# A two-layer hybrid backbone on one core: equal tile addresses modulo 512, plain-order Hyena gates, and a first posts tile partly from SBUF

## The chip, the core and the metric

The kernel runs on one core of a Trainium2 chip. The engines are called PE (TensorE, the matrix engine; PEld is its loading of weights), DVE (VectorE), ACT (ScalarE), POOL (GpSimd) and SP (SyncE, which issues most DMAs). The metric is the device time of one execution in microseconds, as the median of several runs; a trace of one profiled execution shows where it goes.

## The reference

Two layers over 1024 tokens of width 1024, all in float32. Layer 0 has a mixer of two halves with one input and one output projection: RG-LRU heads (512 channels) and order-2 Hyena channels (512). Layer 1 has a Conformer convolution module. Each layer ends in an expert-choice MoE: 16 experts, each takes its top 128 tokens. What the change touches, cut to its core:

```python
# layer 0, mixer
proj = h @ p['w_in']                       # gate | xa_raw | hy (three pieces of 512)
y_a = gelu(gate) * (hs[0] + flip(hs[1]))   # RG-LRU half
u = dwconv1d(hy, ...)                      # short filter, three taps
v, *gates = split(u, 3)
z = v
for o in range(2):
    z = gates[o] * fftconv(z, kf[:, o], filt_bias[o])
out = concat([y_a, z]) @ p['w_out']
# each layer, MoE
xs = h[idx]                                # the 128 tokens of each of 16 experts
y = (silu(xs @ w1) * (xs @ w3)) @ w2 * gates
```

## The kernel before

**Products.** Nearly every product of the kernel is three matmuls: `mm3` (L155 to L158) multiplies a high part and a low part of both operands, hi x hi (L156), hi x lo (L157), lo x hi (L158), each with a stationary tile of 128x128 and a streamed tile of 128x512. `split` (L160 to L162) makes the two parts: ACT casts the high part, DVE subtracts it and leaves the residual. In the trace these lines stand for all their callers, so tiles' names tell them apart: `e` and `th`, `tl` are weights and tokens of the experts, `oh`, `ol` the output projection's weights, `wh`, `wlo` the input projection's and the conformer's. A few products remain plain float32 matmuls (L1275 with `wx` or `w` and `xf`).

**The layer-0 mixer.** `proj` gives one 128-channel piece of the input projection for all 1024 tokens in PSUM. `gate` (two pieces early, two at the mixer's end) applies gelu (L742, ACT), multiplies by the recurrent half (L743, DVE) and stores the piece `ge` to a DRAM tensor `ycd` (L744), rows 0 to 3 of its seven-piece part. `short` does the short filter of a Hyena piece: one ACT row (L786) and two DVE rows (L787, L788). The long convolution of a 128-channel quarter works through a Fourier transform of 1024 = 8 x 128 points: `tok` transposes the piece (PE, L668, eight tiles read with a stride of 8 elements, and two ACT copies `ut`, L669); `hy_fwd` is 16 matmuls and copies `y4` (L615); `hy_st1` eight DVE rows (L622, L623); `hy_mid` an 8-point transform of 16 rows (L584 to L601), the product with the filter's spectrum and its first butterflies (L633 to L640), and the 16 rows again; `hy_inv` 16 matmuls into two PSUM tiles (L651); `hy_gate` two DVE products (L659), which multiply a PSUM tile in order (a, p) by the gate piece `y` read as `q (p a) -> q a p`, a stride of 8 elements, and write the result `zt` with the same stride. Each of the four quarters goes through it twice (order 0, then order 1): sixteen products. The result of order 0 goes through `tok` again, that of order 1 to `ycd` rows 4 to 6; the last quarter's stays in SBUF. The order of the instructions on PE, DVE and ACT comes from a scheduler, from the posts' first tile on from the code.

**The posts.** The output projection runs over eight tiles of 128 tokens. `y_load` (L935) brings seven channel pieces of a tile from `ycd`, `split` makes `th` and `tl` of them (128x896), the eighth piece `zh`, `zl` comes from the last quarter. Tile 0's 48 matmuls are written with the mixer's last steps: load of `yc`, two wide splits of the weights (`wide_hi` L987 on ACT, `wide_lo` L992 on DVE), the last `drain` (inverse and gate), the splits, the remaining wide splits. After each tile's products come DVE rows (L1049, L1050) and the routing's logits; a top-128 sort for the routing runs on DVE behind them. The same posts code serves layer 1, with tiles `sTh` and `sTl`.

**The experts and the end.** 16 experts per layer; an expert gathers its tokens, has three products with 1024x1024 weights, split on the fly, and scatters. `final` adds the last expert's output per token tile (`ohT`, `hi`, `lo`) and applies the last norm; it has small tiles `ss`, `ms`, `rs` of one column each.

**Addresses.** SBUF tiles are laid out by pools in the order in which they are opened. So a small tile's size shifts the start of all that comes behind it, the tiles of the products among them. `route_open` opens the pool with `gates` and `pos`, which stays for the rest of its layer.

Of the kernel before, what the change touches and what calls it, by code (L numbers as in the profile page):

```python
# [9 lines left out]
F32 = mybir.dt.float32  # L10
# [5 lines left out]
OP = mybir.AluOpType  # L16
# [132 lines left out]
class Builder:  # L149
# [141 lines left out]

    def rstd(self, pool, ss, n=1):
        nc = self.nc
        m = pool.tile([128, n], F32, name="ms", tag="ms", bufs=4)
        nc.vector.tensor_scalar(m, ss, 1.0 / D, EPS, op0=OP.mult, op1=OP.add)  # L295
        r = pool.tile([128, n], F32, name="rs", tag="rs", bufs=4)
        nc.gpsimd.tensor_tensor(r, m, self.nh[:, :n], op=OP.pow)  # L297
        return r
# [354 lines left out]

    def hy_gate(self, p, J):
        dst = p.tile([128, D], F32, name="zt", tag="zt", bufs=1)
        zv = dst.rearrange("q (p a) -> q a p", a=8)
        gv = J["gate"].rearrange("q (p a) -> q a p", a=8)
        for h, q in enumerate(J["r"]):
            self.nc.vector.tensor_tensor(zv[:, h * 4:h * 4 + 4], q, gv[:, h * 4:h * 4 + 4], op=OP.mult)  # L659
        return dst  # L660

    def to_tok(self, src, dst):
        nc = self.nc
        for h in range(2):
            q = self.ps.tile([128, 4, 128], F32, name="q", tag="n")
            for j in range(4):
                a = h * 4 + j
                nc.tensor.transpose(q[:, j], src[:, a::8], self.idn)  # L668
            nc.scalar.copy(dst[:, h * 4:h * 4 + 4, :], q)  # L669

    def even_mixer(self, st, so):
# [7 lines left out]
        with ExitStack() as s1, ExitStack() as sl:  # L679
# [57 lines left out]
            def gate(p, ct, tag, n):  # L737
                P = proj(*piece(ct * 128))
                hs = p.tile([128, n], F32, name="hsr", tag=tag, bufs=4 if tag == "cv" else 2)[:, :D]
                nc.sync.dma_start(hs, self.hsd[ct * 128:(ct + 1) * 128, :])  # L740
                ge = p.tile([128, n], F32, name="ge", tag=tag, bufs=4 if tag == "cv" else 2)[:, :D]
                nc.scalar.activation(ge, P, AF.Gelu_apprx_tanh, bias=0.0, scale=1.0)  # L742
                nc.vector.tensor_tensor(ge, ge, hs, op=OP.mult)  # L743
                nc.sync.dma_start(self.ycd[ct * 128:(ct + 1) * 128, :], ge)  # L744

            with ExitStack() as s2:
# [44 lines left out]
            def tok(y):  # L791
                ut = py.tile([128, 8, 128], F32, name="ut", tag="u", bufs=2)
                self.to_tok(y, ut)
                return ut

            pend = []

            def drain():
                J = pend.pop(0)
                self.hy_inv(py, J)  # L800
                z = self.hy_gate(py, J)
                if J["o"] == 0:
                    return tok(z)
                i = J["qd"]
                if i == 3:
                    return z
                nc.sync.dma_start(self.ycd[512 + i * 128:512 + (i + 1) * 128, :], z)

            for i in range(4):
                J0 = dict(o=0, qd=i, u=tok(short(i)))  # L810
                if i == 0:
# [9 lines left out]
                self.hy_mid(py, J0)  # L821
                J0["gate"] = short(4 + i)
                self.fill(4)
                g1 = short(8 + i)
                pend.append(J0)
                J1 = dict(o=1, qd=i, u=drain(), gate=g1)
                self.hy_fwd(py, J1)
# [5 lines left out]
            self.ada_todo = [(1, 2, k) for k in range(8)]  # L833
            for ct in (2, 3):
                gate(py, ct, "cv", D)
            sl.close()
# [8 lines left out]
            with tc.tile_pool(name="pq0", bufs=1, reuse_waits="tile") as pq, \  # L845
                    tc.manual_schedule(engines={mybir.EngineType.PE, mybir.EngineType.DVE, mybir.EngineType.Activation}):
                y = self.y_load(pq, 0, 1)
                th = pq.tile([128, 7, 128], F32R, name="th")
# [7 lines left out]
                z = drain()  # L856
                self.split(th, tl, y)
                self.split(self.zh, self.zl, z)
# [64 lines left out]
    def route_open(self, l, st):  # L923
        tc = self.tc
        self.pr = pr = st.enter_context(tc.tile_pool(name=f"pr{l}", bufs=1, reuse_waits="tile"))
        self.gates = pr.tile([128, NE], F32, name="gates")
        self.pos = pr.tile([128, 8, NE], F32, name="pos")
# [15 lines left out]
    def mix_open(self, l, st, st2):  # L943
# [17 lines left out]
        E.memset(self.R2, 0.0)  # L961
        self.cb = pm.tile([128, NE], F32, name="cb")

# [523 lines left out]
    def ln_stats(self, Y, bst, pc):  # L1487
# [14 lines left out]
        self.ln_last = getattr(op, "ins", op)  # L1502
        rs = pc.tile([128, 16], F32, name="lrs")
        for a, b in ((0, 2), (2, 6), (6, 11), (11, 16)):
# [66 lines left out]
    def final(self, pe, y, g2b, wx):  # L1571
# [8 lines left out]
        for t in range(8):  # L1580
# [13 lines left out]
            j = pe.tile([128, D], F32, name="sa", tag="sa", bufs=1)  # L1594
            ss = pe.tile([128, 1], F32, name="ss", tag="ss", bufs=4)
            nc.scalar.activation(j, z, AF.Square, bias=0.0, scale=1.0, accum_out=ss)
            V.scalar_tensor_tensor(x, z, self.rstd(pe, ss), wx[0][:, 0], op0=OP.mult, op1=OP.mult)  # L1597
            nc.sync.dma_start(self.out[t * 128:(t + 1) * 128, :], x)
# [95 lines left out]
```

## Time and profile before

| | before |
|---|---|
| median of 3 runs | 2282.1 us (2279.15 to 2284.48) |
| the profiled execution | 2282.96 us |
| its span | 2281.2 us |
| mean granted clock of TensorE | 0.963 |

Times within the trace count from the span's start. The stages lie as follows: preparation and the recurrent half to about 300 us, the Hyena quarters from there to 541 us, the posts of layer 0 to about 690 us, its experts from about 700 us, the conformer from about 1290 us, the posts of layer 1 from about 1520 us, its experts from about 1690 us to the end. A busy engine need not be the one that sets a stage's length: that is read from the waits.

### The profile page before, as it was taken

What the parts mean: (1) busy time and instruction counts of PE and PEld (TensorE: products, weight loads), DVE (VectorE), ACT (ScalarE), POOL (GpSimd) and SP (SyncE); (2) the same over time, 40 slices, a digit from 0 to 9 for tenths busy, and PEclk for the clock granted to TensorE, in tenths of its full rate; (3) what the DMA queues carried; (4) which work ended last, traced back from release to release, by engine and by line L of the source; (5) the groups of instructions that cost most, each with busy time, mean ns of one, the idle gap of its engine ahead of it and who ended that gap; (6) DMA issues with size and microseconds to landing.
All of it is one profiled execution on the core that took longest, in us unless ns stands there. A gap on an engine that the chain in (4) does not pass through costs nothing.

```text
span 2281.2 us, 28699 instructions
## 1 busy us (share of the span) xinstructions
PE 2121.9 (93%) x10626; PEld 1654.5 (73%) x10626; DVE 1818.4 (80%) x2874; ACT 1201.7 (53%) x1459; POOL 129.9 (6%) x131
## 2 busy tenths in 40 slices
PE   7999998988967999999999899989689999999997
PEld 5976766757754877878778588877457777777775
DVE  5979799997596989899888624186969898888887
ACT  3658621212214777777777521134247767676774
POOL 0000000000001000000000100010010000000001
PEclk9999998988988999999999899989889999999999
DMA  7241573654848999999998744334779999999974
GB/s 275 110 139 47 188 274 121 230 203 138 306 155 325 367 394 378 394 380 375 396 381 307 244 148 139 120 109 179 261 292 364 388 368 387 373 372 382 370 267 157
DMA packets 210021, 616.09 MB, mean 270 GB/s; under 512 B 27988, under 2 KB 76758, under 8 KB 200089
## 3 DMA queue, kind: packets, MB, share of 16 engines
q1 hardware_dynamic: 198610, 572.84, 66.2%
q0 software_dynamic: 11248, 41.42, 7.3%
q8 instruction: 83, 1.36, 0.2%
q14 instruction: 56, 0.46, 0.1%
q10 hardware_dynamic: 24, 0.01, 0.0%
HBM read 558.62 MB, written 55.61 MB: 269 GB/s over the span
## 4 chain that ended last, share of the span: by engine, by line
PE 63%; DVE 5%; issue 1%; DMA 1%; POOL 0%; ACT 0%; POOLq 0%; ACTq 0%
PE P L156 17%; PE P L158 17%; PE P L157 17%; PE P L1275 6%; PE q L1240 3%; PE q L1415 1%; DMA xs<-h2d,ix 0%; DVE W L909 0%; DVE wx L1597 0%; POOL rs L297 0%; DVE mm L893 0%; DVE Y L1435 0%; PE q L235 0%; DVE h L1059 0%; DVE S L906 0%
## 5 line engine op out<-in xcount | busy, mean ns | idle before, releaser
L162 DVE TENSOR_TENSOR e<-wx,e 128x1024 fp32r<-128x1024 f32 x516 | 617.9, 1223 | 86.9 <-ACT e L161 73.9
L161 ACT CAST e<-wx 128x1024 fp32r<-128x1024 f32 x516 | 540.2, 1051 | 226.1 <-PE P L158 224.1
L156 PE MATMUL P<-e,th 128*128 128x512 f32 x1384 | 562.9, 407 | 0.0
L158 PE MATMUL P<-e,tl 128*128 128x512 f32 x1384 | 543.5, 393 | 0.8 <-DVE tl L162 0.8
L157 PE MATMUL P<-e,th 128*128 128x512 f32 x1384 | 543.2, 392 | 0.0
L157 PEld LDWEIGHTS P<-e,th 128*128 128x128 f32 x1384 | 260.3, 188 | 60.9 <-DVE e L162 3.8
L156 PEld LDWEIGHTS P<-e,th 128*128 128x128 f32 x1384 | 260.1, 188 | 60.8 <-issue 7.2
L158 PEld LDWEIGHTS P<-e,tl 128*128 128x128 f32 x1384 | 259.9, 188 | 59.9 <-DVE tl L162 1.2
L162 DVE TENSOR_TENSOR e<-w,e 128x1024 fp32r<-128x1024 f32 x176 | 211.7, 1223 | 48.8 <-ACT e L161 29.6
L156 PE MATMUL P<-hh,wh 128*128 128x512 f32 x576 | 228.8, 398 | 16.2 <-DVE y L788 12.8
L161 ACT CAST e<-w 128x1024 fp32r<-128x1024 f32 x176 | 183.9, 1051 | 92.7 <-PE P L158 73.4
L157 PE MATMUL P<-hl,wh 128*128 128x512 f32 x576 | 228.9, 397 | 0.4 <-DVE ms L295 0.4
L158 PE MATMUL P<-hh,wlo 128*128 128x512 f32 x576 | 227.6, 396 | 0.1
L156 PEld LDWEIGHTS P<-hh,wh 128*128 128x128 f32 x576 | 108.9, 189 | 49.8 <-issue 23.7
L157 PEld LDWEIGHTS P<-hl,wh 128*128 128x128 f32 x576 | 109.2, 190 | 27.1 <-issue 4.3
L158 PEld LDWEIGHTS P<-hh,wlo 128*128 128x128 f32 x576 | 108.7, 189 | 26.2 <-issue 3.9
L1315 POOL DMA_INDIRECT acc<-yo,ix x31 | 50.7, 1634 | 923.9 <-DVE yo L1314 923.9
L162 DVE TENSOR_TENSOR tl<-q,th 128x512 fp32r<-128x512 f32 x128 | 84.8, 685 | 5.2 <-ACT th L161 4.1
L161 ACT CAST wh<-w 128x1024 fp32r<-128x1024 f32 x16 | 16.7, 1048 | 124.1 <-PE P L157 124.1
L1275 PE MATMUL P<-wx,xf 128*128 128x512 f32 x176 | 79.1, 592 | 0.0
L161 ACT CAST th<-q 128x512 fp32r<-128x512 f32 x128 | 71.8, 587 | 1.7 <-PE q L1240 1.7
L297 POOL TENSOR_TENSOR rs<-ms,nh 128x1 f32<-128x1 f32 x42 | 24.2, 577 | 825.0 <-issue 435.9
(415 smaller groups left out, 3030.0 us busy)
## 6 DMA issues: line engine op xcount, KB each, us to landing
wx<-i_exp_w SPq DMA_DIRECT2D x272, 1024.0 KB, 8.1
w<-i_exp_w SPq DMA_DIRECT2D x96, 1024.0 KB, 7.6
w<-i_w_mod SPq DMA_DIRECT2D x40, 1024.0 KB, 7.8
wst<-i_w_in SPq DMA_DIRECT2D x20, 512.0 KB, 4.4
kd<-w SPq DMA_DIRECT2D x8, 1024.0 KB, 5.0
w<-kd SPq DMA_DIRECT2D x8, 1024.0 KB, 8.6
acc<-res SPq DMA_DIRECT2D x16, 512.0 KB, 2.9
e<-i_exp_w SPq DMA_DIRECT2D x16, 512.0 KB, 7.7
```

The lines of the kernel that those rows point to most:

```text
L156: t.matmul(o, lh, rh, start=start, stop=False)
L157: t.matmul(o, lh, rl, start=False, stop=False)
L158: t.matmul(o, ll, rh, start=False, stop=stop)
L161: self.nc.scalar.copy(hi, src)
L162: self.nc.vector.tensor_sub(lo, src, hi.bitcast(F32))
L297: nc.gpsimd.tensor_tensor(r, m, self.nh[:, :n], op=OP.pow)
L1240: nc.tensor.transpose(q[:, j], src[:, c * 128:(c + 1) * 128], self.idn)
L1275: nc.tensor.matmul(P[:, ns], f[:, k], h[:, ns], start=k == 0, stop=k == 7)
L1315: self.last = nc.gpsimd.indirect_dma_start(self.acc[l][:, :], bass.IndirectOffsetOnAxis(ap=xT[e][1][:, 0:1], axis=0), yo, None, compute_op ...
L1415: op = nc.tensor.matmul(q[64 * half:64 * half + 64, gr % 4], U2[half][:, gr], TT[half][:, gr], start=True, stop=True, tile_position=(0, 64 ...
```

## The change

Three edits stand in one diff.

1. Sizes of small tiles are changed, without a use of what is added: `gates` of layer 1 gets 40 more columns, `cb` 16, `lrs` 120, and the small tiles of `final` move to another ring of buffers. The start addresses behind them shift. The table has, for the streamed and the stationary tile of a product, the difference of their start addresses modulo 512 bytes, from the allocation in either program.

| products | matmuls | before | after |
|---|---|---|---|
| experts of layer 0 (`e`; `th`, `tl`) | 692 x 3 | 0 | 0 |
| experts of layer 1 (`e`; `th`, `tl`) | 692 x 3 | 224 | 0 |
| experts of layer 1, plain float32 (`wx`; `xf`) | 44 | 224 | 0 |
| posts of layer 0, tile 0, and piece 7 of all | 10 x 3 and more | 0 | 0 |
| posts of layer 0, tiles 1 to 7 (`oh`, `ol`; `th`, `tl`) | 98 x 3 | 448 | 0 |
| posts of layer 1 (`oh`, `ol`; `sTh`, `sTl`) | 128 x 3 | 320 | 0 |
| conformer (`wh`, `wlo`; `hh`, `hl`) | | 0 | 0 |

2. The Hyena gate is permuted once by ACT (`hy_perm`, eight copies of 128x1024), so that the gate product reads and writes in plain order. The transposes behind an order-0 product read its result in plain order. For order 1, quarters 0 to 2, ACT copies the result back to the stride-8 order (`zs`, three copies) before its store. The last quarter's order-1 products still write with the stride. Both new tiles share a ring of four buffers with `y`, `ge` and `hsr`.

3. The first posts tile takes pieces 2 and 3 from the SBUF tiles that `gate` returns; the load of `yc` covers pieces 0, 1 and 4 to 6 in two DMAs, and the split is done in four parts (two, one, one and three pieces).

```diff
     def hy_gate(self, p, J):
+        nc = self.nc
         dst = p.tile([128, D], F32, name="zt", tag="zt", bufs=1)
-        zv = dst.rearrange("q (p a) -> q a p", a=8)
-        gv = J["gate"].rearrange("q (p a) -> q a p", a=8)
+        last = J["o"] == 1 and J["qd"] == 3
+        zv = dst.rearrange("q (p a) -> q a p", a=8) if last else dst.rearrange("q (a p) -> q a p", a=8)
         for h, q in enumerate(J["r"]):
-            self.nc.vector.tensor_tensor(zv[:, h * 4:h * 4 + 4], q, gv[:, h * 4:h * 4 + 4], op=OP.mult)
-        return dst
+            nc.vector.tensor_tensor(zv[:, h * 4:h * 4 + 4], q, J["gate"][:, h * 4:h * 4 + 4], op=OP.mult)
+        if J["o"] == 0 or last:
+            return dst
+        z = p.tile([128, D], F32, name="zs", tag="cv", bufs=4)
+        nc.scalar.copy(z.rearrange("q (p a) -> q a p", a=8), zv)
+        return z
+
+    def hy_perm(self, p, y):
+        g = p.tile([128, D], F32, name="ga", tag="cv", bufs=4).rearrange("q (a p) -> q a p", a=8)
+        self.nc.scalar.copy(g, y.rearrange("q (p a) -> q a p", a=8))
+        return g
...
-                nc.tensor.transpose(q[:, j], src[:, a::8], self.idn)
+                nc.tensor.transpose(q[:, j], src[:, a], self.idn)
...
-                J0["gate"] = short(4 + i)
+                J0["gate"] = self.hy_perm(py, short(4 + i))
...
-                J1 = dict(o=1, qd=i, u=drain(), gate=g1)
+                J1 = dict(o=1, qd=i, u=drain(), gate=self.hy_perm(py, g1))
...
-                y = self.y_load(pq, 0, 1)
+                y = pq.tile([128, 7, 128], F32, name="yc")
+                yv = self.ycd.rearrange("(k p) t -> p k t", p=128)[:, :, 0:128]
+                for a, b in ((0, 2), (4, 7)):
+                    nc.sync.dma_start(y[:, a:b], yv[:, a:b])
...
-                self.split(th, tl, y)
+                for a, b, part in ((0, 2, y[:, 0:2]), (2, 3, ges[0][:, None, :128]), (3, 4, ges[1][:, None, :128]), (4, 7, y[:, 4:7])):
+                    self.split(th[:, a:b], tl[:, a:b], part)
...
-        self.gates = pr.tile([128, NE], F32, name="gates")
+        self.gates = pr.tile([128, NE + (40 if l else 0)], F32, name="gates")[:, :NE]
...
-        self.cb = pm.tile([128, NE], F32, name="cb")
+        self.cb = pm.tile([128, 2 * NE], F32, name="cb")[:, :NE]
...
-        rs = pc.tile([128, 16], F32, name="lrs")
+        rs = pc.tile([128, 136], F32, name="lrs")[:, :16]
...
-            ss = pe.tile([128, 1], F32, name="ss", tag="ss", bufs=4)
+            ss = pe.tile([128, 1], F32, name="ss", tag="ix", bufs=6)
...
-            V.scalar_tensor_tensor(x, z, self.rstd(pe, ss), wx[0][:, 0], op0=OP.mult, op1=OP.mult)
+            V.scalar_tensor_tensor(x, z, self.rstd(pe, ss, tag="ix", bufs=6), wx[0][:, 0], op0=OP.mult, op1=OP.mult)
```

In the code of the change lines below the gates stand some ten to seventeen further down (gate product L660, copy-back L664, permutation L669, transposed tile L679, gelu L752, its product L753, short filter L797 to L799, wide splits L1004 and L1009). How the order moves is seen at three places.

DVE at the mixer's end, before. `L600`, `L601` are the last transform rows, `L743` the second gelu product, `L992` the wide residuals, `L659` the last gate pair, `tl` and `zl` the residuals of tile 0.

```order
L600 SCALAR_TENSOR_TENSOR pq<-sub,E 128x2x128
L601 SCALAR_TENSOR_TENSOR pq<-sub,E 128x2x128
L743 TENSOR_TENSOR ge<-ge,hsr 128x1024
L992 TENSOR_TENSOR ol<-w,oh 128x2048 x2
L659 TENSOR_TENSOR zt<-q,y 128x4x128 x2
L162 TENSOR_TENSOR tl<-yc,th 128x896
L162 TENSOR_TENSOR zl<-zt,zh 128x1024
L992 TENSOR_TENSOR ol<-w,oh 128x2048 x2
```

All wide residuals and the second gelu product stand behind the transform there; the first gelu product stood ahead of it.

DVE there with the change, first ahead of the last transform's 16 rows (`L639`, `L640` are the butterflies directly ahead of them).

```order
L753 TENSOR_TENSOR ge<-ge,hsr 128x1024
L637 TENSOR_TENSOR sub<-E,w 128x1024
L1009 TENSOR_TENSOR ol<-w,oh 128x2048
L638 TENSOR_TENSOR pq<-pq,sub 128x8x128
L753 TENSOR_TENSOR ge<-ge,hsr 128x1024
L639 TENSOR_TENSOR E<-pq 128x1024
L640 TENSOR_TENSOR E<-pq 128x1024
```

Both gelu products stand among the rows of the filter product, and one wide residual does. Behind the last transform, on DVE with the change:

```order
L601 SCALAR_TENSOR_TENSOR pq<-sub,E 128x2x128
L1009 TENSOR_TENSOR ol<-w,oh 128x2048
L660 TENSOR_TENSOR zt<-q,ga 128x4x128 x2
L162 TENSOR_TENSOR tl<-yc,th 128x256
L162 TENSOR_TENSOR tl<-ge,th 128x128 x2
L162 TENSOR_TENSOR tl<-yc,th 128x384
L162 TENSOR_TENSOR zl<-zt,zh 128x1024
L1009 TENSOR_TENSOR ol<-w,oh 128x2048 x2
```

One wide residual is left between the transform and the gate pair, and tile 0's residual comes in four parts.

ACT at the mixer's end, before (gelu, wide casts, cast of tile 0).

```order
L286 COPY w<-q 8x256
L742 ACT_TABLE_LOAD
L742 ACTIVATE ge<-P 128x1024 x2
L987 CAST oh<-w 128x2048 x3
L161 CAST th<-yc 128x896
L161 CAST zh<-zt 128x1024
L987 CAST oh<-w 128x2048
```

Both gelu rows stand together, and one row casts tile 0.

The same with the change.

```order
L752 ACT_TABLE_LOAD
L752 ACTIVATE ge<-P 128x1024
L286 COPY w<-q 8x256
L1004 CAST oh<-w 128x2048
L752 ACTIVATE ge<-P 128x1024
L1004 CAST oh<-w 128x2048 x2
L161 CAST th<-yc 128x256
L161 CAST th<-ge 128x128 x2
L161 CAST th<-yc 128x384
L161 CAST zh<-zt 128x1024
L1004 CAST oh<-w 128x2048
```

A wide cast stands between the two gelu rows now, and the cast of tile 0 comes in four parts, of which two read `ge`.

DVE around a gate pair of order 0 in the second quarter, before: the end of a transform, residuals of the weight split (`wlo`), the gate pair, then the rows behind a forward transform.

```order
L600 SCALAR_TENSOR_TENSOR pq<-sub,E 128x2x128
L601 SCALAR_TENSOR_TENSOR pq<-sub,E 128x2x128
L162 TENSOR_TENSOR wlo<-wst,wh 128x1024 x2
L659 TENSOR_TENSOR zt<-q,y 128x4x128 x2
L622 TENSOR_TENSOR pq<-q,y_2877 128x256
```

Two residuals stand between the transform and the gate pair.

The same with the change.

```order
L600 SCALAR_TENSOR_TENSOR pq<-sub,E 128x2x128
L601 SCALAR_TENSOR_TENSOR pq<-sub,E 128x2x128
L799 SCALAR_TENSOR_TENSOR y<-P,vec,y 128x1023
L162 TENSOR_TENSOR wlo<-wst,wh 128x1024
L660 TENSOR_TENSOR zt<-q,ga 128x512 x2
L622 TENSOR_TENSOR pq<-q,y_2887 128x256
```

One of the two `wlo` rows went ahead, and the short filter's second row stands there; the gate pair has the plain form. On ACT the new copies of that quarter stand between the rows of the short filter.

```order
L664 COPY zs<-zt 128x8x128
L797 ACTIVATE y<-P,vec 128x1024
L161 CAST wh<-wst 128x1024
L669 COPY ga<-y 128x1024
L797 ACTIVATE y<-P,vec 128x1024
L669 COPY ga<-y 128x1024
L679 COPY ut<-q 128x512 x2
L615 COPY y_3364<-q 128x256
```

The copy-back `zs` is ahead of a short filter's row, and the permutations `ga` are behind one each, the second of them ahead of the transposed tile. On PE, the inverse of such an order-0 gate had two and two projection matmuls directly ahead of it and has 28 and 13 now, the 13 between its fourth and fifth matmul; this is so in three quarters.

## Rows read from the trace of the kernel before

**Rows 1.** The page, busy time of each engine, share of the span, instructions.

```profile
PE 2121.9 (93%) x10626; PEld 1654.5 (73%) x10626; DVE 1818.4 (80%) x2874; ACT 1201.7 (53%) x1459; POOL 129.9 (6%) x131
```

Columns of a window: its bounds, its length, busy microseconds of each engine with its records, the granted clock of TensorE as a share of full speed, the mean busy share of the DMA engines, and what they moved in GB/s.

**Rows 2.** Windows of twelve experts: layer 0, layer 1; length, then each engine's busy time.

```profile
730.40:1156.40 426.00, 426.00 (x1970) 338.06 (x1969) 385.28 (x372) 312.81 (x336) 30.85 (x24) 1.00 1.01 383
1696.40:2131.40 435.00, 435.00 (x1970) 338.56 (x1969) 385.58 (x373) 312.72 (x336) 30.84 (x24) 1.00 1.01 374
```

A row gives shortest, median and longest duration in ns, and the first and the last start.

**Rows 3.** Timeline of line L1275 on PE, layer 0 then layer 1, grouped.

```profile
L1275 PE MATMUL P<-wx,xf x64: 590/592/592, 730.5 to 1088.5; 128*128 128x512 f32 x64
...
L1275 PE MATMUL P<-wx,xf x64: 591/592/593, 1696.4 to 2061.9; 128*128 128x512 f32 x64
```

A row of this view gives line, engine, operation, output and inputs, shapes, count; then busy microseconds and mean ns of one; then idle time of the engine ahead of it.

**Rows 4.** Groups by form, three-pass matmuls of twelve experts, layer 0 then 1.

```profile
L157 PE MATMUL P<-e,th 128*128 128x512 f32 x528 | 205.9, 390 | 0.0
...
L157 PE MATMUL P<-e,th 128*128 128x512 f32 x529 | 209.0, 395 | 0.0
```

**Rows 5.** Groups by form: layer-0 posts, layer-1 posts, conformer.

```profile
L157 PE MATMUL P<-ol,th 128*128 128x512 f32 x72 | 28.4, 395 | 0.0
...
L157 PE MATMUL P<-ol,sTh 128*128 128x512 f32 x88 | 34.6, 394 | 0.0
...
L157 PE MATMUL P<-hl,wh 128*128 128x512 f32 x122 | 47.6, 390 | 0.0
```

**Rows 6.** Windows of the layer-0 posts, columns as in rows 2.

```profile
570.00:590.00 20.00, 19.94 (x117) 14.79 (x116) 10.48 (x14) 6.34 (x12) 1.10 (x2) 1.00 0.93 309
630.00:650.00 20.00, 19.11 (x101) 14.88 (x101) 19.09 (x99) 3.32 (x6) 0.55 (x1) 1.00 0.40 132
```

**Rows 7.** Windows of the Hyena stage, columns as in rows 2.

```profile
300.00:541.40 241.40, 216.32 (x1238) 162.65 (x1236) 225.21 (x405) 46.84 (x73) 0.00 (x0) 0.94 0.53 191
360.00:380.00 20.00, 11.35 (x49) 9.44 (x49) 17.60 (x27) 0.59 (x1) 0.00 (x0) 0.57 0.42 142
```

**Rows 8.** Groups by form: Hyena gates, a plain PSUM product, an ACT cast.

```profile
L659 DVE TENSOR_TENSOR zt<-q,y 128x512 f32<-128x512 f32 x14 | 15.4, 1121 | 4.7 <-PE q L651 4.7
...
L1049 DVE TENSOR_TENSOR y<-P,g1b 128x512 f32<-128x512 f32 x6 | 4.1, 692 | 15.0 <-PE P L158 14.8
...
L161 ACT CAST wh<-wst 128x1024 fp32r<-128x1024 f32 x10 | 10.5, 1052 | 67.9 <-PE P L157 67.9
```

A row gives who waited and for whom; total microseconds, times, the longest.

**Rows 9.** Waits of DVE, 290 to 565 us.

```profile
DVE pq L622 <- ACT y L615: 9.8, 5, 2.7
DVE zt L659 <- PE q L651: 4.7, 5, 1.3
```

A row gives start, duration, engine, line, operation, and in brackets the engine's idle time before it and what ended that.

**Rows 10.** Timeline of the mixer's end: DVE, PE, ACT, SP's queue.

```profile
541.29 1.22 DVE L743 TENSOR_TENSOR ge<-ge,hsr 128x1024 f32<-128x1024 f32 x1
542.43 4.49 DVE L992 TENSOR_TENSOR ol<-w,oh 128x2048 fp32r<-128x2048 f32 x2
546.83 2.04 DVE L659 TENSOR_TENSOR zt<-q,y 128x512 f32<-128x512 f32 x2
552.51 1.09 DVE L162 TENSOR_TENSOR tl<-yc,th 128x896 fp32r<-128x896 f32 x1 [3.64 <-ACT th L161]
...
541.43 5.02 PE L651 MATMUL q<-IG,pq 128*128 128x128 f32 x28 [2.52 <-DVE pq L601]
552.53 0.80 PE L156 MATMUL P<-oh,th 128*128 128x512 f32 x1 [6.08 <-ACT th L161]
...
558.09 0.63 PE L156 MATMUL P<-oh,th 128*128 128x512 f32 x1
...
565.45 0.39 PE L157 MATMUL P<-ol,zh 128*128 128x512 f32 x1
...
566.36 0.39 PE L158 MATMUL P<-oh,zl 128*128 128x512 f32 x1
...
551.54 0.94 ACT L161 CAST th<-yc 128x896 fp32r<-128x896 f32 x1 [6.63 <-DMA yc<-ycd]
...
547.76 0.37 SPq L935 DMA_DIRECT2D yc<-ycd  x1
```

More of the change, by code (lines that the diff above doesn't have):

```diff
@@ L290, in bcast, with rstd @@
         self.nc.sync.dma_start(dst, self.rowd[l][i:i + 1, :].to_broadcast([128, D]))
-    def rstd(self, pool, ss, n=1):
+    def rstd(self, pool, ss, n=1, tag=None, bufs=4):
         nc = self.nc
-        m = pool.tile([128, n], F32, name="ms", tag="ms", bufs=4)
+        m = pool.tile([128, n], F32, name="ms", tag=tag or "ms", bufs=bufs)
         nc.vector.tensor_scalar(m, ss, 1.0 / D, EPS, op0=OP.mult, op1=OP.add)
-        r = pool.tile([128, n], F32, name="rs", tag="rs", bufs=4)
+        r = pool.tile([128, n], F32, name="rs", tag=tag or "rs", bufs=bufs)
         nc.gpsimd.tensor_tensor(r, m, self.nh[:, :n], op=OP.pow)
@@ L744, in gate @@
                 nc.sync.dma_start(self.ycd[ct * 128:(ct + 1) * 128, :], ge)
+                return ge
             with ExitStack() as s2:
@@ L794, in tok, with split8 @@
                 return ut
+            def split8(y):
+                return y.rearrange("q (p a) -> q a p", a=8)
             pend = []
@@ L802, in drain @@
                 if J["o"] == 0:
-                    return tok(z)
+                    return tok(z.rearrange("q (a p) -> q a p", a=8))
                 i = J["qd"]
@@ L809, in even_mixer @@
             for i in range(4):
-                J0 = dict(o=0, qd=i, u=tok(short(i)))
+                J0 = dict(o=0, qd=i, u=tok(split8(short(i))))
                 if i == 0:
@@ L833, in even_mixer @@
             self.ada_todo = [(1, 2, k) for k in range(8)]
-            for ct in (2, 3):
-                gate(py, ct, "cv", D)
+            ges = [gate(py, ct, "cv", D) for ct in (2, 3)]
             sl.close()
```

## The prediction

> **What bounds the kernel now.** I read the busy line of the page first: PE is busy 2121.9 us of the 2281.2 us span, so a gain has to shorten PE's work or one of the stretches in which PE waits [rows 1]. Then I went through the three stretches that the change touches.
>
> The experts are PE alone: in twelve expert periods of either layer PE is busy 426.00 of 426.00 us and 435.00 of 435.00 us, at granted clock 1.00, with the same 1970 matmul records, DVE and ACT below and the DMA engines equally occupied [rows 2]. Yet layer 1 takes 9.0 us more, 0.75 us per expert. A matmul that comes once per period tells the same: ten periods are 1088.5 - 730.5 = 358.0 us in layer 0 and 2061.9 - 1696.4 = 365.5 us in layer 1 [rows 3]. The excess sits in the three-pass matmuls, whose mean is 390 ns in layer 0 and 395 ns in layer 1 [rows 4], while the plain float32 matmuls have 592 ns in both [rows 3]. By the tile addresses of the program, the streamed tile and the stationary tile start 0 bytes apart modulo 512 in layer 0 and 224 apart in layer 1.
>
> The Hyena stage (300 to 541.4 us) is DVE's: 225.21 us busy of 241.40, PE 216.32, ACT only 46.84, granted clock 0.94 [rows 7]. At the mixer's end DVE, the y load and PE hand over to each other, row by row [rows 10]. The posts behind it are PE's at first (19.94 of 20 us) and then as much DVE's, because of the sort (19.09 us in 630 to 650) [rows 6].
>
> The profiled execution took 2282.96 us, span 2281.2; the median of the runs is 2282.1. I sum against 2282.96; the 0.9 us between the two is small beside the terms.
>
> **A. Layer-1 experts.** Padding takes the difference of their 692 x 3 three-pass matmuls from 224 to 0, what layer 0 has. 16 experts x 0.75 us = 12.0 us [rows 2]. By matmuls: 9.0 us over the 1586 of the twelve periods is 5.7 ns each, and 2076 of them make 11.8 us. Behind the last expert stands the final loop, in which PE is not alone, so I take **11.5** (10.5 to 12.0). Is it the difference of addresses, though? Three other stretches run the same three-pass form. The conformer's products, with difference 0, have a mean of 390 ns; the posts of layer 0, 448 apart, 395; those of layer 1, 320 apart, 394 [rows 5]. Four stretches out of four sort by it.
>
> [...]
>
> **B. Posts.** In layer 0, 42 of a tile's 48 three-pass matmuls go from 448 apart to 0 (tile 0 has 0 already), in layer 1 all 48 go from 320 to 0. At 5 ns and 4 ns by rows 5 that is 0.2 us per tile. From about the fifth tile on, DVE's sort sets the pace and hides it, which leaves four tiles of each layer: 4 x 0.21 + 4 x 0.19 = **1.6** (0 if DVE hides all, 3 if none).
>
> **C. Hyena gates.** 14 of the 16 gate products read the gate and write the result in plain order. Strided they take 1121 ns; a product of the same 128x512 with a PSUM operand in plain order takes 692 [rows 8]. 14 x 0.429 = **6.0** us off DVE, which is the busy engine here. The bounds are 0, if a PSUM operand costs here what the stride did, and 6.0. The last pair stays strided.
>
> What is added is eleven 128x1024 copies on ACT with a stride on one side. No row shows one; a cast of that size in plain order takes 1.05 us [rows 8], and with the DVE rows' ratio 1121/692 it would be an estimated 1.70, so 11.6 to 18.7 us. I take 1.7 each. ACT has 46.84 of 241.40 us in use [rows 7], so it has room. What counts is who is behind a copy in ACT's queue. Behind the copy of the gate stand the two copies of the transposed tile, but they wait for a gate product and eight transposes anyway; behind the copy-back (order 1) stand the short filter's ACT row and then DVE's row on it, with transform rows of DVE in between. Hidden: 0. Without that cover it costs three turns x 1.7 = 5.1 us.
>
> The order in these turns changes too. DVE's sixteen idle microseconds are mostly two waits: 9.8 us on the y4 copies behind a forward transform, 4.7 us of a gate product on PE's inverse [rows 9]. In the new order PE has projection matmuls (28 and 13) around the first inverse matmuls of three turns in place of two and two, and one residual product of the weight split and the short filter's second row stand ahead of the gate. The gate's wait should shrink; what stood behind the gate as filling for the y4 wait is gone from there. I take a net gain of **1.0**, between a gain of 5 (the 4.7 and a little) and a loss of 4 (some half of the 9.8 once more).
>
> **D. The end of the mixer.** Before: the last transform row ends at 541.3, then DVE has a gelu product, two wide residuals and the gate pair; the y load is issued only at 547.76, since it waits for the store of the second gelu product, its cast starts at 551.54 and PE at 552.53, so PE waits 6.08 us after the inverse [rows 10]. PE then does 46 + 2 matmuls of tile 0; its last starts at 566.36 and ends at 566.75. [...]
>
> After: one gelu product and one wide residual (1.14 + 2.25 = 3.4 us) go ahead of the last transform, so it ends at 544.7 on the old scale. The inverse takes 5.0 (546.45 - 541.43) and ends at 549.8; the remaining wide residual lies beside it. The second gate product ends at 550.9. Rows 2 and 3 of the y tile come from SBUF and the others from stores that are long done, so the casts stand ready; the first residual, two of the seven pieces, takes some 0.4 of the 1.09 us that the seven take now [rows 10], to 551.3. PE starts then with 46 matmuls to go: at 0.2275 that is 10.5 us, to 561.8 or 562.2 with the first steps slower. Gain **4.6**. [...] Tile 1's load waits for PE to have read tile 0's tiles, so it moves along, and so does all behind it.
>
> **Final loop.** A ring of six for three small tiles looks two tiles ahead rather than four: 0 to 1 us of loss, taken as 0.
>
> **Sum:** 11.5 + 1.6 + 6.0 + 1.0 + 4.6 = 24.7; 2282.96 - 24.7 = 2258.3. So **2258 us**.
>
> **Rivals.**
> 1. *Addresses do nothing* (layer 1 is slower for another reason, its output traffic say). For: nothing in the trace shows the mechanism. Against: four stretches sort by it, and the two expert layers have the same work. A and B go: 2258.3 + 13.1 = 2271.4. 8%.
> 2. *PE takes over the Hyena stage.* PE is 216 us busy against DVE's 219 once 6 are gone, so DVE may just wait longer for PE's inverse and y4. C goes, the 1.0 with it: 2258.3 + 7.0 = 2265.3. 13%.
> 3. *The inverse and the gate take the place of the y load.* [...] 12%.
> 4. *Slower.* [...] 2%.
> 5. *Better.* [...] 10%.
>
> My forecast has the remaining 55%. **Range** 2250 to 2268: it holds the forecast with its bounds and rivals 2, 3 and 5, and leaves out 1 and 4 and some edges, under 2 in 10. A difference of 0.2% (4.6 us) is about what a measurement of this kernel can tell. Faster by more than that: 0.95 (the forecast and rivals 1, 2, 3 and 5); within it 0.03, where rival 1 meets rival 2; slower 0.02.
>
> **What would show it.** A: a layer-1 expert period of 35.5 us and a three-pass mean of 390 ns; 36.25 and 395 prove rival 1. B: post means of 390. C: gate products near 0.69 us, PE's clock above 0.94 in the stage; a longer wait of DVE for the inverse or y4 means rival 2. An ACT copy of over 3 us, or DVE waiting for ACT's short row, means the cover was wrong. [...] The forecast is wrong as a whole if 5 ns per matmul belongs to layer 1 and not to the addresses.

## The result and the profile after

| | before | changed |
|---|---|---|
| median | 2281.53 us (4 runs) | 2266.49 us (4 runs, 2263.99 to 2268.93) |
| ratio | | 0.9932, 95% interval 0.9919 to 0.9945 |
| the profiled execution, its span | 2282.96, 2281.2 us | 2268.93, 2267.2 us |

The change gains 15 us, within the range, but 8 us short of the forecast of 2258. So two things are to be explained: where the 15 come from, and where the rest of the 24.7 went. The page of the changed kernel, busy time of each engine, answers to [rows 1]:

```profile
PE 2108.0 (93%) x10626; PEld 1649.9 (73%) x10626; DVE 1811.0 (80%) x2877; ACT 1226.3 (54%) x1473; POOL 129.9 (6%) x131
```

PE lost 13.9 us of work, DVE 7.4; ACT has 25 more. Rows of DVE that both traces have tell where the 14.0 us of span arise; the lead is how much earlier a row starts with the change.

| up to this row of DVE | before | changed | lead | gained here | forecast |
|---|---|---|---|---|---|
| first row behind the first forward transform | 280.90 | 278.35 | 2.55 | 2.55 | none |
| first product on tile 0 of the posts | 566.11 | 561.03 | 5.08 | 2.5 | 11.6 (C, order, D) |
| first split of layer 1's expert weights | 1674.02 | 1670.70 | 3.32 | -1.8 | 1.6 (B) |
| last gated row of the experts (`sa<-sa,P`) | 2238.56 | 2223.86 | 14.70 | 11.4 | 11.5 (A) |
| last row (its end) | 2275.83 | 2261.81 | 14.02 | -0.7 | 0 |

The first 2.55 us aren't the change's: PE and DVE run the same instructions up to there, ACT has one copy more (`ga`, 2.19 us, done 5 us ahead of the first `y4` copy), 2 us of the lead are there already at 150 us, and other executions below start that row anywhere from 275.6 to 284.5. Single traces carry that much luck; it is kept apart in what follows.

**Experts.** The three views of [rows 2 to 4] for layer 1 with the change: a window of twelve experts (columns as there), the timeline of the matmul that comes once per period, and the group of one kind of three-pass matmuls.

```profile
1692.90:2118.90 426.00, 426.00 (x1969) 338.11 (x1968) 384.34 (x373) 313.33 (x336) 30.85 (x24) 1.00 1.02 382
...
L1292 PE MATMUL P<-wx,xf x64: 590/592/592, 1692.9 to 2050.9; 128*128 128x512 f32 x64
...
L157 PE MATMUL P<-e,th 128*128 128x512 f32 x528 | 205.9, 390 | 0.0
```

Layer 1 has become layer 0: 426 us instead of 435, ten periods in 358.0 us instead of 365.5, a mean of 390 ns instead of 395.

**Hyena stage.** The gate products, the two kinds of new copies, and DVE's waits (290 to 545 us), to be held against [rows 8, 9]:

```profile
L660 DVE TENSOR_TENSOR zt<-q,ga 128x512 f32<-128x512 f32 x14 | 9.5, 687 | 4.7 <-PE q L651 4.7
...
L669 ACT COPY ga<-y 128x1024 f32<-128x1024 f32 x7 | 14.9, 2132 | 47.2 <-issue 31.3 <-DVE y L799 15.9
...
L664 ACT COPY zs<-zt 128x1024 f32<-128x1024 f32 x3 | 6.6, 2189 | 13.4 <-DVE zt L660 13.4
...
DVE pq L622 <- ACT y L615: 18.7, 7, 6.0
DVE zt L660 <- PE q L651: 4.7, 7, 1.4
```

The products fell from 1121 to 687 ns, the 6.0 us that were forecast. But the wait for the y4 copies rose from 9.8 to 18.7 us. The wait is longest at one place; DVE there, before and with the change:

```profile
409.53 1.28 DVE L787 SCALAR_TENSOR_TENSOR y<-P,vec,y 128x1023 f32<-128x1023 f32 x1
...
410.85 1.28 DVE L788 SCALAR_TENSOR_TENSOR y<-P,vec,y 128x1023 f32<-128x1023 f32 x1
412.05 1.22 DVE L162 TENSOR_TENSOR wlo<-wst,wh 128x1024 fp32r<-128x1024 f32 x1
415.80 0.42 DVE L622 TENSOR_TENSOR pq<-q,y 128x256 f32<-128x256 f32 x1 [2.53 <-ACT y L615]
```

```profile
404.95 0.42 DVE L601 SCALAR_TENSOR_TENSOR pq<-sub,E 128x256 f32<-128x256 f32 x1
405.29 0.16 DVE L278 SCALAR_TENSOR_TENSOR gg<-mod,vec 128x8 f32<-128x8 f32 x1
...
411.50 0.42 DVE L622 TENSOR_TENSOR pq<-q,y 128x256 f32<-128x256 f32 x1 [6.05 <-ACT y L615]
```

Before, a short filter's two rows and a residual fill the time behind the transform, and 2.53 us remain. Now that work has been done earlier, and DVE stands idle for 6.05 us. PE in the same stretch, with the change (transposes of the short filter's piece, projection matmuls, modulation products, the forward transform):

```profile
393.81 1.33 PE L678 MATMUL q<-idn,y 128*128 128x128 f32 x8 [2.60 <-DVE y L799]
...
406.60 0.39 PE L157 MATMUL P<-hl,wh 128*128 128x512 f32 x1
...
407.14 2.78 PE L235 MATMUL q<-w,sp 128*32 128x512 f32 x24
409.85 3.84 PE L612 MATMUL q<-ut,G 128*128 128x128 f32 x32
```

The transform L612 had its input a little after 395, but 44 projection matmuls of the next piece and 24 records of modulation products stand ahead of it. That queue isn't new. Before, 46 projection matmuls and the same 24 records stood there:

```profile
411.44 2.78 PE L235 MATMUL q<-w,sp 128*32 128x512 f32 x24
414.15 3.84 PE L612 MATMUL q<-ut,G 128*128 128x128 f32 x32
```

What is new is that DVE has nothing left to do while PE works through it.

**Mixer's end**, to [rows 10]: PE, ACT, SP's queue.

```profile
544.25 5.26 PE L651 MATMUL q<-IG,pq 128*128 128x128 f32 x28 [3.07 <-DVE pq L601]
549.26 0.48 PE L156 MATMUL P<-oh,th 128*128 128x512 f32 x1
549.58 0.40 PE L157 MATMUL P<-ol,th 128*128 128x512 f32 x1
550.96 0.50 PE L158 MATMUL P<-oh,tl 128*128 128x512 f32 x1 [0.98 <-DVE tl L162]
...
540.64 0.51 ACT L161 CAST th<-yc 128x384 fp32r<-128x384 f32 x1 [2.35 <-DMA yc<-ycd]
...
536.74 0.36 SPq L863 DMA_DIRECT2D yc<-ycd  x1
```

The y load is issued 11 us earlier, the casts are done ahead of the inverse, and PE waits 0.98 us where it waited 6.08.

### The profile page after: what moved, and what is told of

Read it like the earlier page. It is cut to its first block, busy times and chain, and to the rows that moved or that the text cites. A ratio compares the mean times of both kernels' runs of the same rounds, so it can differ in the third digit from the quotient of the medians.

```text
span 2267.2 us, 28722 instructions
## 1 busy us (share of the span) xinstructions
PE 2108.0 (93%) x10626; PEld 1649.9 (73%) x10626; DVE 1811.0 (80%) x2877; ACT 1226.3 (54%) x1473; POOL 129.9 (6%) x131
## 4 chain that ended last, share of the span: by engine, by line
PE 78%; DVE 12%; DMA 3%; ACT 3%; issue 3%; POOL 1%; SPq 0%; POOLq 0%; ACTq 0%; DVEq 0%
PE P L156 20%; PE P L158 20%; PE P L157 20%; PE P L1292 6%; PE q L1257 3%; PE q L235 2%; PE q L612 1%; PE q L651 1%; PE q L1432 1%; DMA wx<-i_exp_w 1%; PE q L529 1%; PE q L413 1%; DMA w<-i_w_mod 1%; POOL rs L297 1%; PE q L326 1%
## 5 line engine op out<-in xcount | busy, mean ns | idle before, releaser
L156 PEld LDWEIGHTS P<-e,th 128*128 128x128 f32 x1384 | 260.1, 188 | 57.4 <-issue 7.2
```

The lines of the kernel that those rows point to most:

```text
L156: t.matmul(o, lh, rh, start=start, stop=False)
```

## The experiments

Ratios are to the kernel before on the same chip. Beside them stands, from each run's trace, the length of *stage and end*: from DVE's first row behind the first forward transform to its first product on tile 0. It leaves out the luck of the first 280 us. It is 285.2 us before and 282.7 with the change.

| run | ratio, 95% | stage and end |
|---|---|---|
| changed | 0.9932 (0.9919 to 0.9945) | 282.7 |
| pads | 0.9955 (0.9942 to 0.9968) | 283.7 |
| gates | 1.0002 (0.9993 to 1.0011) | 284.5 |
| first | 0.9970 (0.9961 to 0.9979) | 280.0 |
| nogates | 0.9930 (0.9916 to 0.9943) | 280.2 |
| shift0 | 1.0000 (0.9991 to 1.0009) | 285.7 |
| noact | 0.9915 (0.9902 to 0.9929) | 275.2 |
| copies | 0.9939 (0.9925 to 0.9952) | 280.3 |
| fwdfirst, fwdfirst2 | 0.9926 (0.9913 to 0.9940), 0.9914 (0.9900 to 0.9927) | 276.7, 279.1 |
| ng_fwdfirst | 0.9955 (0.9941 to 0.9969) | 284.7 |
| apart224 | 0.9990 (0.9981 to 0.9999) | 280.1 |
| apart32 | 1.0003 (0.9993 to 1.0012) | 280.7 |

### Each part alone, and the change without its gates

**pads**: the sizes of small tiles and the ring of the final loop alone.

```diff
-        self.gates = pr.tile([128, NE], F32, name="gates")
+        self.gates = pr.tile([128, NE + (40 if l else 0)], F32, name="gates")[:, :NE]
```

> The kernel before with the padding of the small tiles alone (gates of layer 1, cb, lrs, and the ring of the final loop); gates and first tile as before, the order of the instructions unchanged but for the last rows of the final loop. Address theory: a layer-1 expert falls from 36.25 to 35.5 us, together 11 to 12 us; the posts give nothing, since the sort behind them sets their end: 2281.5 - 11.5 = 2270 us. Rival (layer 1 is slower for another reason): no change, 2281 us.

10 us gained (0.9955), and ten periods of layer 1 in 358.0 us. It came as expected.

```profile
L1275 PE MATMUL P<-wx,xf x64: 590/592/592, 1696.6 to 2054.6; 128*128 128x512 f32 x64
```

**gates**: `hy_perm`, the plain `hy_gate` and its copy-back, the plain transposes alone.

```diff
-                J0["gate"] = short(4 + i)
+                J0["gate"] = self.hy_perm(py, short(4 + i))
```

> The kernel before with the plain-order gates alone (permutation and copy-back on ACT, plain transposes); addresses and first tile as before. Theory: the order of the Hyena turns that comes with it gives the 6 us of the products back in the wait behind the forward transforms (18.7 us as in the changed kernel, 9.8 before), so the stage is no shorter; but the second gelu product now stands ahead of the last transform, so the y load no longer ends last at the mixer's end, which is worth some 3 to 5 us: 2277 to 2279 us. Rival (the loss in the Hyena stage comes with the new addresses or the ring of buffers shared with the first tile's edit): the stage is 5 us shorter, and with the mixer's end 2272 us.

No gain at all (1.0002). The wait for the y4 copies is 18.7 us here too, with the addresses of before; so the order that comes with the gates brings it, not the pads.

```profile
DVE pq L622 <- ACT y L615: 18.7, 7, 6.0
```

The 3 to 5 us hoped for at the mixer's end don't show in the time. In the trace they are there: from the end of the last transform to the first product on tile 0 it takes 18.2 us, and 3.4 us of work have moved ahead of it, against 24.7 before, so 3.1 are gained. But the stretch up to that transform is longer by 2.4 beyond the moved work.

**first**: tile 0 from SBUF and in four parts alone.

```diff
-                self.split(th, tl, y)
+                for a, b, part in ((0, 2, y[:, 0:2]), (2, 3, ges[0][:, None, :128]), (3, 4, ges[1][:, None, :128]), (4, 7, y[:, 4:7])):
+                    self.split(th[:, a:b], tl[:, a:b], part)
```

> The kernel before with the first posts tile's edit alone (two pieces from SBUF, split in four); its order is that of before everywhere else, so both gelu products keep their places. Theory: the residual of tile 0 starts right behind the gate pair at 548.9 instead of 552.5 us, a gain of 3 to 4 us: 2278 us. Rival (the gain at the mixer's end needs the gelu product ahead of the transform): under 1 us, 2281 us.

More than expected: 0.9970, some 7 us by the median and 5.2 by stage and end. DVE and PE at its mixer's end:

```profile
546.72 2.04 DVE L659 TENSOR_TENSOR zt<-q,y 128x512 f32<-128x512 f32 x2
548.66 0.42 DVE L162 TENSOR_TENSOR tl<-yc,th 128x256 fp32r<-128x256 f32 x1
...
541.32 3.39 PE L651 MATMUL q<-IG,pq 128*128 128x128 f32 x28 [2.53 <-DVE pq L601]
545.14 0.50 PE L156 MATMUL P<-oh,th 128*128 128x512 f32 x1 [0.43 <-ACT th L161]
...
549.14 0.50 PE L158 MATMUL P<-oh,tl 128*128 128x512 f32 x1 [3.26 <-DVE tl L162]
```

The residual follows the gate pair at 548.66 as worked out, 3.85 us ahead of [rows 10]; the rest is PE's: two matmuls of tile 0 are done ahead of the residual, and from 553.1 us on the starts are 0.23 us apart (0.43 in the seven steps from 549.72 to 552.71), where those of [rows 10] are 0.46 apart from 552.53 to 558.09 (twelve steps, granted clock 0.50 in 552.5 to 558.1 us). The second gelu product didn't have to move.

**nogates**: the change without the gate edit.

> The changed kernel without its gate edit: padding and first tile, gates as before. Theory (the gate edit is worth nothing or less, as its saving comes back as waits): 2281.5 - 11.5 - 3.5 = 2266.5 us, no slower than the changed kernel. Rival (the gates do bring their 6 us, and the profile of the changed kernel shows a disturbed stretch): 2271 to 2273 us, 5 us slower than the changed kernel.

0.9930: what pads and first give together, and the same as the whole change. The gate edit is worth nothing on top of them.

### Are the gates' 6 us real?

**noact**: the change with plain products but no copies (the Hyena half computes other values). Its order is nearly that of nogates.

```diff
-        g = p.tile([128, D], F32, name="ga", tag="cv", bufs=4).rearrange("q (a p) -> q a p", a=8)
-        self.nc.scalar.copy(g, y.rearrange("q (p a) -> q a p", a=8))
-        return g
+        return y.rearrange("q (a p) -> q a p", a=8)
```

> The changed kernel without its eleven ACT copies: the gate products read and write in plain order, but nothing is permuted, so the Hyena half computes other values. The order of its instructions is nearly that of the kernel without the gate edit. Theory (the saving on DVE is real, and it is the order brought by the copies that gives it back): the order of before with shorter products, 5 to 6 us below the kernel without the gate edit, 2261 us. Rival (PE and the hand-overs between the engines set the stage whatever the order, so shorter products only make DVE wait): the same 2266.5 us.

5.0 us less than nogates in stage and end, of which 3.3 lie ahead of the end of the last transform and 1.7 behind it; 0.9915 against 0.9930 in time (some 3.4 us, the intervals overlap). The windows from the first row to the end of the last transform, changed kernel, nogates, noact, columns as in [rows 2]:

```profile
278.35:544.20 265.85, 236.16 (x1346) 172.48 (x1344) 239.69 (x438) 75.06 (x92) 0.00 (x0) 0.94 0.56 204
...
280.70:541.30 260.60, 235.26 (x1345) 174.34 (x1344) 242.63 (x436) 49.05 (x77) 0.00 (x0) 0.94 0.56 201
...
282.70:540.00 257.30, 233.54 (x1345) 173.13 (x1344) 236.65 (x436) 49.16 (x77) 0.00 (x0) 0.95 0.56 205
```

DVE's work falls by 6.0 us from nogates to noact, and the stretch by 3.3: idle time rises from 18.0 to 20.7. In the changed kernel 3.4 us of DVE's work from behind the transform lie in the stretch too, but idle time is 26.2, 8.2 above nogates. One trace is little to go by, but several runs share an order of instructions. The same stretch in all of them:

| order | traces | stretch, us | DVE busy | DVE idle |
|---|---|---|---|---|
| of before | before, pads, first, nogates, shift0 | 260.4 to 260.7 | 242.6 to 242.7 | 17.8 to 18.2 |
| of before, shorter products | noact | 257.3 | 236.7 | 20.7 |
| of the change | changed, gates, apart224, apart32 | 265.9, 266.2, 262.8, 263.5 | 239.6 to 239.8 | 26.2, 26.4, 23.2, 23.9 |
| of fwdfirst | fwdfirst, fwdfirst2 | 258.8, 261.2 | 236.4 | 22.4, 24.8 |

Five traces of the old order lie within 0.3 us, and noact is 3 us below them. So the saving is real, and about half of it reaches the stretch in the old order. In the order of the change 5 to 8 us are waited instead: about all of it, and the changed kernel's own trace is one of the two worse ones.

**copies**: the copies kept, the products strided again (other values too).

```diff
-        zv = dst.rearrange("q (p a) -> q a p", a=8) if last else dst.rearrange("q (a p) -> q a p", a=8)
+        zv = dst.rearrange("q (p a) -> q a p", a=8)
```

> The changed kernel with its eleven ACT copies kept and the gate products strided again on both sides (the Hyena half computes other values). Theory (the copies bring the bad order, and the products' 6 us count on top of it): 4 to 6 us above the changed kernel, 2271 to 2273 us, with a wait of DVE for the y4 copies near 18 us. Rival (copies are hidden, PE sets the stage): within 1 us of the changed kernel, 2266 us.

Neither theory: 0.9939, 1.6 us above the changed kernel, with overlapping intervals, and a y4 wait of 7.6 us, not 18, but 6.2 us on the short filter's ACT row. The scheduler had chosen yet another order. So copies don't bring one fixed order, and this run doesn't separate their own time from the order.

**fwdfirst**: in the changed kernel the four modulation products of quarters 2 to 4 stand behind the forward transform.

```diff
-                else:
-                    self.fill(4)
                 self.hy_fwd(py, J0)
                 self.hy_st1(py, J0)
+                if i:
+                    self.fill(4)
```

> The changed kernel with one move: the four filling products of the modulation weights stand behind the forward transform of order 0 and its first DVE rows, not ahead of them, in quarters 2 to 4; the scheduler then issues that transform right behind the transposes, ahead of some 44 projection matmuls. Theory (the y4 wait of 18.7 us comes from projection matmuls that stand ahead of the forward transform on PE): the wait falls by 5 us or more, and the kernel to about 2261 us. Rival (PE has no slack, so these matmuls are only late elsewhere): 2266 us, with the wait moved to the inverse or to the short filter's rows.

The transform now follows the transposes at once, and DVE its own last transform row, without a wait (PE, then DVE):

```profile
396.34 1.05 PE L678 MATMUL q<-idn,y 128*128 128x128 f32 x8
...
397.62 3.84 PE L612 MATMUL q<-ut,G 128*128 128x128 f32 x32
...
404.47 0.41 DVE L601 SCALAR_TENSOR_TENSOR pq<-sub,E 128x256 f32<-128x256 f32 x1
404.80 0.41 DVE L622 TENSOR_TENSOR pq<-q,y 128x256 f32<-128x256 f32 x1
```

The y4 waits fall to 13.8 us, stage and end from 282.7 to 276.7. The median, 0.9926, shows little of it. The wait isn't where most of this comes from, either: in this order the second gelu product and the wide residual (3.4 us) stand behind the last transform again. With that work counted behind it in both, the stretch is 258.8 us against 262.4 in the changed kernel, 259.4 in apart224 and 260.1 in apart32, and the mixer's end 17.9 against 20.2, 20.7 and 20.6.

**fwdfirst2**: the same kernel again, for its time.

> The kernel of fwdfirst once more, for its time: its trace had a stage 6 us shorter than the changed kernel's, its median only about 1 us below, with some 3 us of spread from the program's first 280 us. Theory: it is faster than the changed kernel by 3 to 6 us, a ratio to before of 0.990 to 0.992. Rival: the shorter stage was a property of that one execution, 0.993.

0.9914, stage and end 279.1. The y4 wait is 13.9 us again, but the gate products wait 6.7 us for the inverse (4.7 in the changed kernel), so a part of the wait has only moved, as the rival of fwdfirst had it. The order of the changed kernel has three traces (apart224 and apart32 share it): 282.7, 280.1 and 280.7, mean 281.2; this one has 276.7 and 279.1, mean 277.9. It is likely some 3 us faster than the changed kernel and the quickest of the kernels that do all the work, but the intervals of the ratios overlap, so that isn't settled.

**ng_fwdfirst**: the same move without the gate edit.

> The changed kernel without its gate edit (strided products, no copies), with the filling products behind the forward transform as in the run fwdfirst. Theory (with the transform early on PE, DVE's own work sets the stage, so the products' 6 us count): stage and mixer's end 4 to 6 us longer than the 276.7 us of fwdfirst, near 281 us. Rival (PE and the hand-overs set the stage): 277 us like fwdfirst.

284.7 us, longer even than expected, but this isn't the products alone: its order has one wait of 7.2 us on the short filter's ACT row that none of the others has. Inconclusive on the products; it shows once more what a single wait of one order can cost.

### Is it the addresses, and which?

**shift0**: 56 columns more in the gates tile of layer 0, in the kernel before.

> The kernel before with one pad: the gates tile of layer 0 (not of layer 1) gets 56 more columns, so that the experts of layer 0, whose streamed and stationary tiles start 0 apart modulo 512, are 224 apart like those of layer 1 before (their posts go from 448 to 160 apart). Instructions and order are unchanged. Address theory: a layer-0 expert rises from 35.5 to 36.25 us, 11 to 12 us in all, 2295 us, three-pass mean 395 ns in both layers. Rival (layer 1 is slower for a reason of its own, and the pads' gain comes from something else there): 2283 us, layer 0 stays at 390 ns.

No change (1.0000), but the test had failed: by the allocation the pad had not moved the experts' tiles of layer 0 against each other (they are still 0 apart). It only moved the posts' from 448 to 160.

**apart224** and **apart32**: the changed kernel with a small unused tile ahead of layer 0's expert weights, and more columns in layer 1's gates (here of apart224).

```diff
+        if l == 0:
+            self.nc.gpsimd.memset(self.pw.tile([128, 56], F32, name="padw"), 0.0)
...
-        self.gates = pr.tile([128, NE + (40 if l else 0)], F32, name="gates")[:, :NE]
+        self.gates = pr.tile([128, NE + (104 if l else 0)], F32, name="gates")[:, :NE]
```

> The changed kernel with other addresses and nothing else (one unused tile of 56 columns in the pool of the streamed expert weights of layer 0, one GpSimd memset; 64 more columns in the gates tile of layer 1): experts of layer 0 are 224 bytes apart modulo 512, those of layer 1 256. The earlier try with a pad in layer 0 had not moved those tiles, by the allocation. Address theory (only equal addresses are free): layer 0 as slow as layer 1 was, 233 ns from one three-pass matmul to the next and 12 us more, and layer 1 slower too by 8 to 12 us: 2287 to 2291 us. If the rule goes by 256 rather than 512, layer 1 stays fast: 2278 us. Rival (layer 1 had another reason): 2266.5 us, 227 ns in both.

> The same with 8 columns in layer 0 and 16 in layer 1: streamed and stationary tiles of the experts are 32 bytes apart in layer 0 and 64 in layer 1. Theory (any difference modulo 512 costs the same): 233 ns in both layers, 2266.5 + 24 = 2290 us. Alternative (a small difference costs less, the cost grows with the distance): 228 to 230 ns and 2270 to 2278 us. Rival: 2266.5 us.

The timeline of the matmul that comes once per period, over 14 periods: apart224 layer 0 (224 apart) and layer 1 (256), then apart32 layer 0 (32) and layer 1 (64).

```profile
L1294 PE MATMUL P<-wx,xf x88: 591/592/593, 724.6 to 1234.6; 128*128 128x512 f32 x88
...
L1294 PE MATMUL P<-wx,xf x88: 590/592/592, 1701.9 to 2201.4; 128*128 128x512 f32 x88
```

```profile
L1294 PE MATMUL P<-wx,xf x88: 592/592/593, 721.7 to 1231.8; 128*128 128x512 f32 x88
...
L1294 PE MATMUL P<-wx,xf x88: 590/592/593, 1698.9 to 2201.6; 128*128 128x512 f32 x88
```

Layer 0 before, with 0 apart:

```profile
L1275 PE MATMUL P<-wx,xf x88: 590/592/592, 730.5 to 1230.0; 128*128 128x512 f32 x88
```

From 499.5 us it rises to 510.0 and 510.1 once its tiles are apart. That is the cause shown in both directions. But layer 1 at 256 apart takes 499.5, as fast as at 0, and 502.7 at 64. The medians from one three-pass matmul's start to PE's next, worked out from the starts in the traces over all such matmuls of a stretch, gaps over 320 ns left out:

| apart modulo 512 | modulo 256 | ns | where |
|---|---|---|---|
| 0 | 0 | 227 | experts, conformer, posts with the change |
| 256 | 0 | 227 | apart224, experts of layer 1 |
| 64 | 64 | 229 to 231 | apart32, experts of layer 1 |
| 320 | 64 | 229 to 231 | posts of layer 1 before |
| 448 | 192 | 233 to 234 | posts of layer 0 before |
| 224 | 224 | 233 to 234 | experts of layer 1 before; apart224 |
| 160 | 160 | 234 to 235 | shift0, posts of layer 0 |
| 32 | 32 | 234 | apart32, experts of layer 0 |

Every row fits a rule modulo 256, with 64 dearer than 0 by a third to a half of what the others cost (3.2 of 10.5 us over the 14 periods). 96 and 128 were not tried. Nor is it one tile's own start: by the allocation, modulo 512, the streamed tile of layer 0's experts starts alike in the changed kernel, apart224 and apart32, and the stationary one moves; in layer 1 it is the other way round. In time apart224 came to 2280.9 us, 3 above the 2278 of a rule by 256, and apart32 to 2284.3, between its two theories.

## Why the prediction was right or wrong, point by point

- **A, right**: 11.4 us against 11.5, from the cause named, the addresses. *Addresses do nothing* is refuted by pads and apart224. Too narrow was the unit: equality modulo 256 was enough (227 ns at 256 apart in apart224, 233 to 234 at 224). Why the addresses matter isn't shown.
- **B, wrong in size**: 1.6 forecast, nothing seen. The gaps did shorten (from 233 to 227 ns in layer 0), but the lead falls by 1.8 us from tile 0 to layer 1's experts, and in nogates it is 5.23 at tile 0 and 5.18 at the start of them. Most likely the sort sets the posts' end altogether (DVE is busy 18.8 to 19.1 of every 20 us from 620 to 680 in the changed kernel, PE 4.0 in the last 20); the step that let four tiles of each layer count was the failing one, and its lower bound of 0 was the answer.
- **C, the failing term**: 6.0 forecast for the products, 6.0 measured on DVE (1121 to 687 ns), and lost as waiting. What failed is the step on the order: *a net gain of 1.0, between a gain of 5 and a loss of 4*. The y4 wait alone grew by 8.9 us (8.7 to 8.9 in the four traces of this order), more than twice the bound. The prediction saw that the filling behind the gate was gone, and bounded it by half the old wait; it didn't follow PE to see what stands ahead of the forward transform, which is what ends that wait: some 45 projection matmuls in either order, most of which DVE's filling had covered before.
- **Rival 2** named the right place and nearly the time (2265.3). The range holds 2266.5 because it was drawn round this rival too; the forecast's own sum missed by 8 us. That PE alone sets the stage isn't shown: it is busy 236 of 265.9 us, and shorter products in the old order (noact) shorten the stretch by 3.3 us. But fwdfirst doesn't refute the rival: its y4 wait falls by 4.9 us, DVE's idle time only to 22.4 and 24.8. The stage reads as a chain of hand-overs in which the order counts; what holds it once the y4 wait is shorter stays open.
- **The copies** cost 2.13 and 2.19 us, above the estimate of 1.70 from DVE's ratio. The waits show none of DVE on the short filter's row in the changed kernel, so the cover held. What they cost beyond the order isn't separated.
- **D, right in size**: from the end of the last transform to the first product on tile 0 it was 24.7 us before and is 16.8, less 3.4 for the work moved ahead: 4.5 gained, 4.6 forecast (4.0 and 4.1 in apart224 and apart32). In part for another reason than written: first alone gets 5 with the gelu product left in its place, and gates alone, which moves that product, gets 3 there. The two don't add up. The 0.2275 us of a matmul in D's sum is the step of the last starts in [rows 10] (565.45 to 566.36, four steps, granted clock 1.00); the 0.4 us for slower first steps is the author's estimate and no run shows it: with the change the first steps behind the residual took 0.33 and 0.24 us. PE stood idle for 10.66 us ahead of the inverse's first matmuls, and the inverse took 5.26 us at granted clock 0.62 (544.25 to 549.51), against 5.02 at 0.66 (541.43 to 546.45) in [rows 10] and 3.39 in first; but the matmuls of tile 0 start 0.23 us apart from 551.3 us on (granted clock 1.00), where those of [rows 10] took 0.46 up to 558.09. Rivals 3 to 5 reckon with paces of PE that are the author's estimates and that no run shows; the paces measured at the mixer's end are these.
- **Final loop**: 0.7 lost, inside the 0 to 1.

## What to carry to other kernels

Where two stretches run the same instructions at different speeds, compare the addresses of their tiles: a pad of some bytes was worth 10 us here, and it is proved by making the fast stretch slow (499.5 to 510.0 us in apart224). A shorter row on the busiest engine is worth what the next wait leaves of it (here 6.0 us of DVE's work, and a ratio of 1.0002 in gates); if a scheduler sets the order, read first what the other engines have queued ahead of the thing that this engine will wait for, and what work it has left to fill that time, and measure the new order with the old durations and the old order with the new ones. Test the parts of a combined change singly: here a third of it, the largest edit in code, gave nothing.

## What the runs showed of the hardware

- Three-pass matmuls of 128x128 by 128x512 with their streamed and stationary tiles at start addresses equal modulo 256 bytes followed each other in 227 ns (before, changed, apart224; granted clock 1.00 in the experts' windows of before and changed); 32 (apart32), 160 (shift0), 192 (before) or 224 apart (before, apart224) in 233 to 235; 64 apart (before, apart32) in 229 to 231. The plain float32 matmuls (`wx`, `xf`) took 590 to 593 ns, 0 apart as well as 224.
- A ScalarE copy of 128x1024 float32 with a step of 32 bytes on one side took 2.13 to 2.19 us (`ga`, `zs`), twice the 1.05 us of a plain cast (`wh`); on VectorE the same stride on both sides made a PSUM product 1.6 times as long (1121 against 687 ns).
